# A two-layer hybrid backbone kernel: the list scheduler orders the instructions by its other model of times

## The chip, the cores and the metric

The kernel runs on one core of a Trainium2 chip. The metric is the device time of one execution in microseconds (us), as the median of several runs; lower is better. The engines are TensorE (PE; its weight loads are shown as PEld), VectorE (DVE), ScalarE (ACT) and GpSimd (POOL). Transfers are issued by SyncE (SP) and, for a few, by POOL. Each engine works through its own list of instructions in the order of the list, and so does the issue queue of SP.

## The reference

Two layers of a token backbone, one sample, 256 context tokens and 256 latent tokens, 1024 channels, all in fp32. Shortened:

```python
def trunk_layer(x_ctx, x_lat, c, c_ctx, ..., need_ctx, p):
    mod_lat = silu(c) @ w_mod + b_mod          # six rows: sh1, sc1, g1, sh2, sc2, g2
    mod_ctx = silu(c_ctx) @ w_mod + b_mod
    u = concat([x_ctx * (1 + sc1c) + sh1c, x_lat * (1 + sc1) + sh1])
    z_a, z_b, z_c, z_d = split_cols(u @ w_in)
    branches = (rwkv7_mixer(z_a), retention_mixer(z_b), hgrn2_mixer(z_c), gqa_mixer(z_d))
    merged = sum(sigmoid(u_rows @ w_gate[i]) * (branches[i] @ w_branch[i]) for i in range(4))
    mix = merged @ w_out
    x_lat = layer_norm(alpha * x_lat + g1 * mix[latent], ln1_g, ln1_b)
    ffn_lat = expert_choice_ffn(x_lat * (1 + sc2) + sh2, w_router, w_e1, w_e3, w_e2)
    x_lat = layer_norm(alpha * x_lat + g2 * ffn_lat, ln2_g, ln2_b)
    ...                                        # layer 0: the same for x_ctx
```

`expert_choice_ffn` lets each of 16 experts take its best tokens (a softmax of the router's logits, top-k), runs silu(x w_e1) * (x w_e3) through w_e2 and adds the results back. Layer 0 keeps all 512 tokens, layer 1 ("last") only the 256 latent ones. Each layer reads 192 MB of expert weights.

## The kernel before, in words

A Python program (class `Block`, called from `hybrid_block`) traces about 14,500 instructions, layer after layer. In a layer the stages follow one another: the modulation rows (`mod_product`, L261: a weight piece of 512 KB, `mw` or `y0`/`y1`, times the condition `sct`; in layer 0 half of the first row's products go to the tile `mod` and half to `m`); the projections and softmax attention, retention and HGRN (matmuls into `pj`, `g`, `y`; weights come by `wload`, L242, as `wr`, and are split by ACT and DVE or POOL into a high and a low half, `wh` and `wl`, for three-pass matmuls); RWKV, a long chain of small matmuls that need ACT and DVE between them, with a filler: the matmuls of the merge (`m<-mh,wh`, `m<-mh,wl`, `m<-ml,wh`) of the branches 3, 2, 1 and of the gate of branch 0, which a table of hooks (FILL) lets into the trace at chosen places of the chain.

The tail of a mixer is what the argument turns on. Its steps, with the names of layer 0 and, behind a slash, of layer 1: the last RWKV outputs (`y<-ar,st`), the group norm (`g<-y,cst` for mean, `g<-cst,sq` for variance), the transposes `g<-ident,rx`; from those the branch's output `y`, which ACT rounds to `yh` for the last merge (`m<-yh,wh`). With the transposes RWKV's buffers come free, and into them go the loads of w_out (`rows_in`, issued by POOL), of the residual `x`, of the router's weights `wrt` and of the first expert weights. Modulation rows are spread over the tokens by matmuls (`w<-rows,ident`), the router's constants are made from `wrt` (DVE: `wrb`, `wrr`) by `w_5948<-wrr` / `w_14246<-wrr`; then comes the last merge (`merge_last`), and the output projection (`h<-oh,mh`), logits, top-k and a gather.

The experts stream: one SP transfer per 1 MB unit (L1569), into a ring of rooms called ring, mid, low, late (and pair in layer 1). A room is refilled when the matmuls that read it are done, and SP issues its list in order, so a transfer whose room isn't free holds back all those behind it.

What sets the order: every instruction is traced in program order with its dependencies; `tile.TileContext` then plays the program against a model of how long each instruction takes and issues, for each engine, the earliest-traced instruction that the model calls ready. Tiles, buffers and addresses are fixed by the program; only the order of each engine's list comes from the model.

## Time and profile before

| | us |
|---|---|
| median of 3 runs | 2302.59 (2302.35 to 2312.79) |
| the profiled execution | 2311.96 |
| its span (1.76 lie outside it) | 2310.2 |
| PE busy in the span | 2048.9 |
| DVE, ACT, POOL busy | 1041.0, 627.2, 268.1 |
| granted TensorE clock, mean | 0.929 |

The profiled execution is 9.37 us above the median; it belongs with the slowest of the three runs. Times inside the execution are read from its trace, in us from the start of the span. A line such as "PE m L201" is an instruction recorded at line 201, which is a helper that all matmuls share, so stages are told apart by time and by tile name. An fp32 matmul shows as two records, an fp32r one as one.

### The profile page before, as it was taken

What the parts mean: (1) busy time and instruction counts of PE and PEld (TensorE: products, weight loads), DVE (VectorE), ACT (ScalarE), POOL (GpSimd) and SP (SyncE); (2) the same over time, 40 slices, a digit from 0 to 9 for tenths busy, and PEclk for the clock granted to TensorE, in tenths of its full rate; (3) what the DMA queues carried; (4) which work ended last, traced back from release to release, by engine and by line L of the source; (5) the groups of instructions that cost most, each with busy time, mean ns of one, the idle gap of its engine ahead of it and who ended that gap; (6) DMA issues with size and microseconds to landing.
All of it is one profiled execution on the core that took longest, in us unless ns stands there. A gap on an engine that the chain in (4) does not pass through costs nothing.

```text
span 2310.2 us, 37585 instructions
## 1 busy us (share of the span) xinstructions
PE 2048.9 (89%) x15964; PEld 1275.7 (55%) x15964; DVE 1041.0 (45%) x2179; ACT 627.2 (27%) x1039; POOL 268.1 (12%) x190
## 2 busy tenths in 40 slices
PE   6999999999999989999999899999889888766775
PEld 3657847677877744333332555868889654222222
DVE  3557755855532536222222557848664642010112
ACT  3353435422222212000000444555343320000000
POOL 2000111233332000000000200103353000000000
PEclk8999999999999989999999899998899988787777
DMA  8354242112124588999999646214222899999996
GB/s 317 97 194 155 64 142 73 41 58 70 56 66 184 201 351 326 422 425 425 426 426 425 220 138 211 69 47 165 92 93 86 338 372 424 424 425 423 424 425 288
DMA packets 96936, 554.85 MB, mean 240 GB/s; under 512 B 11296, under 2 KB 13280, under 8 KB 46848
## 3 DMA queue, kind: packets, MB, share of 16 engines
q1 hardware_dynamic: 95024, 541.83, 60.1%
q0 software_dynamic: 1200, 8.52, 0.9%
q8 instruction: 125, 2.05, 0.3%
q10 hardware_dynamic: 544, 2.10, 0.2%
q14 instruction: 43, 0.35, 0.0%
HBM read 549.13 MB, written 3.28 MB: 239 GB/s over the span
## 4 chain that ended last, share of the span: by engine, by line
PE 63%; DMA 22%; DVE 10%; ACT 2%; issue 2%; POOL 1%; SPq 0%; DVEq 0%; ACTq 0%; POOLq 0%
PE pj L201 14%; PE m L201 13%; PE h L201 12%; PE y L201 9%; DMA late<-in_w_e_dram 8%; PE g L201 6%; DMA mid<-in_w_e_dram 4%; DMA ring<-in_w_e_dram 4%; DMA pair<-in_w_e_dram 3%; PE mod L201 3%; PE w L201 3%; DMA mw<-in_wmod_dram 1%; DMA y<-in_wmod_dram 1%; DVE kb L186 1%; PE w L206 1%
## 5 line engine op out<-in xcount | busy, mean ns | idle before, releaser
L211 POOL TENSOR_TENSOR wl<-wr,wh 128x1280 fp32r<-128x1280 f32 (+1 forms) x62 | 177.7, 2867 | 292.6 <-ACT wh L183 266.2
L183 ACT ACTIVATE wh<-wr 128x1024 fp32r<-128x1024 f32 (+1 forms) x126 | 143.4, 1139 | 190.0 <-PE pj L201 86.4
L201 PE MATMUL m<-mh,wh 128*128 128x512 f32 (+1 forms) x512 | 183.4, 358 | 7.7 <-ACT th L183 7.7
L201 PE MATMUL m<-mh,wl 128*128 128x512 f32 (+1 forms) x512 | 179.4, 350 | 1.0 <-POOL wl L211 1.0
L201 PE MATMUL m<-ml,wh 128*128 128x512 f32 (+1 forms) x512 | 179.0, 350 | 0.0
L201 PE MATMUL h<-late,later 128*32 128x256 f32 (+1 forms) x880 | 143.1, 561 | 28.5 <-DMA late<-in_w_e_dram 28.5
L196 DVE SCALAR_TENSOR_TENSOR h<-h 128x512 f32<-128x512 f32 (+1 forms) x32 | 17.7, 555 | 313.9 <-ACT h L183 313.9
L211 DVE TENSOR_TENSOR wl<-wr,wh 128x1024 fp32r<-128x1024 f32 (+1 forms) x64 | 79.2, 1240 | 109.3 <-ACT wh L183 104.6
L183 ACT ACTIVATE h<-h 128x512 f32<-128x512 f32 (+1 forms) x32 | 15.7, 491 | 401.8 <-PE h L201 401.8
L201 PEld LDWEIGHTS m<-mh,wh 128*128 128x128 f32 x512 | 101.0, 197 | 25.7 <-ACT th L183 9.4
L186 DVE TENSOR_TENSOR h<-h 128x512 f32<-128x512 f32 (+1 forms) x32 | 17.7, 554 | 211.3 <-PE h L201 211.3
L201 PE MATMUL h<-ring,later 128*32 128x256 f32 (+1 forms) x640 | 93.6, 540 | 19.9 <-DMA ring<-in_w_e_dram 19.9
L201 PEld LDWEIGHTS m<-mh,wl 128*128 128x128 f32 x512 | 100.6, 196 | 13.8 <-issue 1.7
L201 PEld LDWEIGHTS h<-late,later 128*32 128x32 f32 (+1 forms) x880 | 45.5, 138 | 112.6 <-issue 63.4
L201 PEld LDWEIGHTS m<-ml,wh 128*128 128x128 f32 x512 | 100.8, 197 | 11.5 <-issue 1.6
L183 ACT ACTIVATE ht<-w 128x512 f32<-128x512 f32 (+1 forms) x32 | 15.7, 491 | 277.4 <-PE w L206 277.4
L201 PE MATMUL y<-late,ht 128*32 128x256 f32 (+1 forms) x536 | 73.5, 501 | 9.5 <-DMA late<-in_w_e_dram 6.9
L201 PE MATMUL h<-mid,later 128*64 128x512 f32 (+1 forms) x352 | 65.6, 569 | 9.0 <-DMA mid<-in_w_e_dram 9.0
L201 PEld LDWEIGHTS h<-ring,later 128*32 128x32 f32 (+1 forms) x640 | 30.1, 136 | 74.1 <-DMA ring<-in_w_e_dram 33.5
L201 PE MATMUL y<-ring,ht 128*32 128x256 f32 (+1 forms) x448 | 62.3, 526 | 9.7 <-DMA ring<-in_w_e_dram 6.3
L183 ACT ACTIVATE th<-m 128x512 f32<-128x512 f32 (+1 forms) x50 | 24.6, 492 | 164.6 <-PE m L201 164.6
L201 PE MATMUL pj<-mh,wl 128*128 128x512 f32 x152 | 61.9, 407 | 0.0
(629 smaller groups left out, 4480.5 us busy)
## 6 DMA issues: line engine op xcount, KB each, us to landing
late<-in_w_e_dram SPq DMA_DIRECT2D x144, 1024.0 KB, 19.5
ring<-in_w_e_dram SPq DMA_DIRECT2D x109, 1024.0 KB, 19.7
mid<-in_w_e_dram SPq DMA_DIRECT2D x63, 1024.0 KB, 19.7
pair<-in_w_e_dram SPq DMA_DIRECT2D x36, 1024.0 KB, 19.6
wr<-in_wmg_dram SPq DMA_DIRECT2D x48, 640.0 KB, 3.9
mw<-in_wmod_dram SPq DMA_DIRECT2D x48, 512.0 KB, 5.0
y<-in_wmod_dram SPq DMA_DIRECT2D x48, 512.0 KB, 4.0
low<-in_w_e_dram SPq DMA_DIRECT2D x20, 1024.0 KB, 19.8
```

Source lines behind the costliest of these rows:

```text
L183: self.nc.scalar.activation(out=out, in_=in_, func=func, **kw)
L186: self.nc.vector.tensor_tensor(out, a, b, op)
L196: self.nc.vector.scalar_tensor_tensor(out, a, s, b, op0, op1)
L201: self.nc.tensor.matmul(out, lhsT, rhs, start=start, stop=stop)
L206: self.nc.tensor.transpose(out, in_, self.ident[b:b + n, b:b + n])
L211: (eng or self.nc.vector).tensor_tensor(lo, src, hi.bitcast(F32), ALU.subtract)
```

## The change

One keyword at the place where the scheduler is made:

```diff
-    with tile.TileContext(nc) as tc:
+    with tile.TileContext(nc, schedule_with_timeline_sim=True) as tc:
```

With it the scheduler uses another model of the instruction times. The compiled program has the same instructions with the same names, operands and addresses (PE 10502, DVE 2141, POOL 195, SP 657 in both, ACT 1019 before and 1017 now, two activation-table loads fewer); what differs is the order of each engine's list, nearly everywhere a little. Three places matter below.

The first is SP's list in the experts of layer 0, where the weights of expert 3 are asked for. Before:

```order
L1569 DMA late6_7270<-in_w_e1_dram 128x2048
L1569 DMA late7_7272<-in_w_e1_dram 128x2048
L1569 DMA ring4_7274<-in_w_e1_dram 128x2048
L1569 DMA ring0_7276<-in_w_e3_dram 128x2048
L1569 DMA ring1_7278<-in_w_e3_dram 128x2048
L1569 DMA mid0_7280<-in_w_e3_dram 128x2048
L1569 DMA mid1_7282<-in_w_e3_dram 128x2048
```

Now:

```order
L1569 DMA late6_7270<-in_w_e1_dram 128x2048
L1569 DMA mid0_7280<-in_w_e3_dram 128x2048
L1569 DMA mid1_7282<-in_w_e3_dram 128x2048
L1569 DMA mid2_7284<-in_w_e2_dram 128x2048
L1569 DMA mid3_7286<-in_w_e2_dram 128x2048
L1569 DMA low0_7288<-in_w_e2_dram 128x2048
L1569 DMA late0_7290<-in_w_e2_dram 128x2048
L1569 DMA late7_7272<-in_w_e1_dram 128x2048
L1569 DMA ring4_7274<-in_w_e1_dram 128x2048
```

The six units into mid, low and late0, whose rooms the first matmuls of expert 2 leave, now stand ahead of late7, ring4, ring0 and ring1, whose rooms the second matmuls of experts 0 and 1 leave.

The second is PE's list at the tail of layer 0's mixer, a piece of the difference (`rx`: the normed RWKV output; `m_6119`, `m_6225`: merge matmuls of the gate and of the last merge; `w_5948`: the router's constants).

```order
 L201 MATMUL m_6119<-mh_109,wh_6115 128x512
 L201 MATMUL m_6119<-ml_110,wh_6115 128x512
+L206 MATMUL g_5861<-ident_91,rx_5839 128x128 x4
+L206 MATMUL g_5866<-ident_91,rx_5839 128x128 x4
 L201 MATMUL m_6119<-mh_109,wl_6116 128x512
...
 L201 MATMUL m_6225<-yh_6212,wh_6221 128x512
+L201 MATMUL w_5948<-wrr_5938,one_97 128x64
 L201 MATMUL m_6225<-yl_6211,wh_6221 128x512
```

Before, the transposes stood in the middle of the merge `m_5959` and the router's step in `m_6023`, five and four merges earlier; between the two stand now 53 merge matmuls and four `w<-rows` steps, before 42 and four.

The third is PE's list at the tail of layer 1's mixer. Before, around the transposes:

```order
L201 MATMUL m_14283<-ml_11007,wh_14279 128x256
L201 MATMUL m_14283<-mh_11006,wl_14280 128x256
L201 MATMUL m_14315<-mh_11006,wh_14311 128x256
L201 MATMUL m_14315<-ml_11007,wh_14311 128x256
L206 MATMUL g_14138<-ident_91,rx_14120 128x128 x2
L206 MATMUL g_14141<-ident_91,rx_14120 128x128 x2
L201 MATMUL m_14315<-mh_11006,wl_14312 128x256
L201 MATMUL m_14315<-mh_11006,wh_14311 128x256
```

Now:

```order
L201 MATMUL m_14379<-mh_11006,wl_14376 128x256
L201 MATMUL g_14121<-y0_8833,cst_9041 128x256
L201 MATMUL g_14129<-cst_9041,sq0_14118 128x2
L201 MATMUL g_14129<-cst_9041,sq1_14119 128x2
...
L206 MATMUL g_14138<-ident_91,rx_14120 128x128 x2
L206 MATMUL g_14141<-ident_91,rx_14120 128x128 x2
L201 MATMUL m_14419<-yh_14406,wh_14415 128x256
L201 MATMUL m_14430<-yh_14406,wh_14415 128x256
L201 MATMUL w_14212<-rows_9740,ident_91 32x256 x4
...
L201 MATMUL w_14225<-rows_9531,ident_91 128x512
...
L201 MATMUL w_14246<-wrr_14240,one_97 128x32
L201 MATMUL m_14419<-yl_14405,wh_14415 128x256
```

The gate's merges (`m_14315` to `m_14379`), which stood behind the transposes, now all stand ahead of the norm, and norm, transposes, the first use of `yh` and the router's step follow one another directly.

## Rows read from the trace of the kernel before

**Rows 1.** The page: the chain that ended last, by engine, share of the span.

```profile
PE 63%; DMA 22%; DVE 10%; ACT 2%; issue 2%; POOL 1%; SPq 0%; DVEq 0%; ACTq 0%; POOLq 0%
```

**Rows 2.** Busy time by stretch: stretch, length, engines (instructions), granted clock, DMA share, GB/s.

```profile
0.00:79.00 79.00, 58.81 (x325) 42.46 (x325) 29.91 (x64) 23.15 (x38) 13.46 (x19) 0.91 0.66 249
79.00:690.00 611.00, 589.76 (x4816) 420.45 (x4814) 363.21 (x729) 237.28 (x374) 111.31 (x70) 0.99 0.29 92
690.00:834.00 144.00, 125.01 (x585) 99.88 (x587) 65.92 (x133) 43.34 (x64) 14.99 (x8) 0.92 0.55 219
834.00:1276.00 442.00, 418.39 (x1924) 151.57 (x1922) 123.83 (x238) 38.50 (x70) 0.12 (x1) 1.00 0.99 407
1276.00:1780.00 504.00, 469.68 (x4508) 368.05 (x4505) 329.86 (x729) 222.25 (x371) 117.35 (x81) 0.95 0.37 122
1780.00:1863.00 83.00, 65.20 (x383) 52.20 (x381) 51.80 (x106) 32.48 (x53) 10.87 (x11) 0.88 0.79 316
1863.00:2310.20 447.20, 322.01 (x3432) 141.13 (x3432) 76.43 (x183) 30.21 (x71) 0.00 (x0) 0.77 0.96 401
```

**Rows 3.** The chain in order of time: start, us, what; ends of both expert stages.

```profile
1254.93 20.15 DMA late<-in_w_e_dram
...
1876.05 18.41 DMA mid<-in_w_e_dram
```

**Rows 4.** PE's longest waits: 79 to 330, 330 to 690, 1560 to 1780; total, times, longest.

```profile
PE mod L201 <- DMA y<-in_wmod_dram: 4.9, 4, 2.3
...
PE m L201 <- ACT th L183: 2.8, 1, 2.8
...
PE m L201 <- ACT th L183: 4.9, 3, 2.3
```

**Rows 5.** PE in order of time at layer 0's tail; idle before and releaser in brackets.

```profile
683.87 1.04 PE L206 MATMUL g<-ident,rx 128*128 128x128 f32 x8
...
691.37 1.98 PE L201 MATMUL w<-rows,ident 128*128 128x512 f32 x4 [1.69 <-ACT g L183]
...
704.35 0.66 PE L201 MATMUL w<-wrr,one 128*128 128x64 f32 x2 [3.98 <-DVE wrr L1443]
```

**Rows 6.** The same place by stretch, and two stretches of layer 0's experts.

```profile
706.00:711.00 5.00, 5.00 (x14) 3.88 (x14) 0.00 (x0) 0.00 (x0) 0.00 (x0) 0.56 0.49 197
711.00:735.00 24.00, 24.00 (x108) 19.85 (x107) 0.53 (x1) 7.73 (x10) 9.57 (x4) 1.00 0.44 175
880.00:916.00 36.00, 35.23 (x176) 15.51 (x178) 23.76 (x44) 4.30 (x8) 0.00 (x0) 1.00 0.78 289
916.00:1255.00 339.00, 321.34 (x1462) 110.40 (x1456) 85.95 (x166) 22.16 (x37) 0.12 (x1) 1.00 1.01 424
```

**Rows 7.** All engines in order of time at layer 1's tail.

```profile
1773.49 0.68 PE L201 MATMUL y<-ar,st 64*64 64x64 f32 x16
...
1781.33 0.70 PE L201 MATMUL g<-y,cst 128*128 128x256 f32 x2
...
1787.05 0.60 PE L206 MATMUL g<-ident,rx 128*128 128x128 f32 x4
...
1795.63 0.42 ACT L183 ACTIVATE yh<-y 128x256 fp32r<-128x256 f32 x1 [2.89 <-DVE y L186]
...
1797.74 0.36 DVE L1443 TENSOR_REDUCE wrr<-wrt 128x16 f32<-128x128 f32 x1
...
1820.02 0.80 PE L201 MATMUL h<-oh,mh 128*128 128x512 f32 x1 [3.10 <-ACT oh L183]
```

**Rows 8.** The start: SP's issues and the products that use the late ones.

```profile
19.47 8.81 SPq L261 DMA_DIRECT2D mw<-in_wmod_dram  x8
29.19 0.33 SPq L1753 DMA_DIRECT2D cst<-in_cst_dram  x1
...
36.86 2.97 SPq L261 DMA_DIRECT2D y<-in_wmod_dram  x2
...
44.94 3.63 PE L201 MATMUL m<-mw,sct 128*32 128x512 f32 x16
```

## The prediction

> **What bounds the kernel now.** I read the chain that ended last first: 63% of it is PE work and 22% transfers [rows 1]. Then busy time by stretch, since those shares mix stages [rows 2]. In both mixers PE is the bound: from 79 to 690 it works 589.76 of 611 us, from 1276 to 1780 469.68 of 504. A new order can't shorten that work, only the 21.2 and 34.3 us of idle time in it. From 834 to 1276, the experts of layer 0, both are near their end: PE works 418 of 442 us and the transfers fill 0.99 of the time; PE's own work then stops at 1254.93 and the last 20.15 us of the stage are a transfer [rows 3]. From 1863 on the transfers alone decide (0.96 of the time, PE 322 of 447 us), and the chain there is one row of transfers of some 20 us [rows 2, 3]. So a microsecond won or lost before 1863 moves the end by a microsecond, and inside layer 1's experts no order of the engines buys anything as long as the transfers follow each other without a gap. Between the stages lie two tails (690 to 834 and 1780 to 1863) where PE is idle for 19.0 and 17.8 us; they are chains through ACT, DVE and new loads.
>
> The question is therefore where PE's idle time goes, and whether a gap in the stream of weights closes. Instruction counts and sizes are the same, so there is no cost or gain of work except two activation-table loads on ACT, an engine that is busy for 27% and that I cost at nothing because PE or the transfers cover it.
>
> **The start.** SP's eight second transfers of the first modulation row (issued from 19.47) now stand behind cst, rot, gq, three rows of biases and constants, y0, y1 and one `wr`, which before were issued behind them, from 29.19 to 39.83 [rows 8]: up to 10.6 us later. PE in turn has all its other ready projections ahead of their products, which before ran in between and ended at 48.57 [rows 8]. The last issue was at 28.28; at 38.9 it would be in flight as long as the `y` pair, some 7 us, and its product would end about 2 us late. Two products of y0 and y1 behind it fill a later wait. I take +2 us, from 0 to +5.
>
> **The mixers.** In layer 0's attention PE waits 4.9 us in four places for `y` pieces of modulation weights [rows 4]. The new order spreads these products singly among projections where before they came in pairs, so the next load is asked for sooner; I take half, -2, with 0 and -4.9 as ends. In RWKV the long waits are for ACT (`th`, 2.8 us in layer 0 and 4.9 in three places in layer 1) [rows 4], with DVE's behind them. The new lists put more merge matmuls (0.22 us each, 108 in 24 us [rows 6]) ahead of a number of these chain steps. They also use them up: a merge that is moved ahead isn't there later, and I see steps set right behind their producers too. I take -3 in layer 0 and -4 in layer 1, where the idle time is the larger; the ends are zero and half of the idle time in each mixer, -10 and -17.
>
> **The tail of layer 0.** Transposes at 683.87; router's step at 704.35 after a wait of 3.98 us, and another wait of 1.69 us for a modulation row at 691.37 [rows 5]. The wait is followed by a granted clock of 0.56 from 706 to 711, in which 14 matmuls take the 5 us that 22 or so take afterwards [rows 6]; it costs some 2 us. In all 5.67 + 2, about 7.7 us. In the new order the 20.5 us from the transposes to the router's step (the load of `wrt` is issued when RWKV's buffers come free and lands behind larger loads) must be covered by 53 matmuls at 0.22 and four `w` steps, of which two took 1.98 [rows 5]: 11.8 + about 4 = 16 us. Some 4 us of waiting are left, instead of 7.7, and the modulation rows now have their inputs long before. I take -4. Ends: -7.7 (the load lands earlier, since nothing else is asked for there) and +3 (the wait is followed by the low clock again and the last merge is late).
>
> **Experts of layer 0.** From 880 to 916 the transfers move 289 GB/s, from 916 to 1255 424 [rows 6]: 36 x (1 - 289/424) = 11.5 us of transfer time are lost, because late7 and what stands behind it wait for rooms that experts 0 and 1 leave with their second matmuls. Now the six units into mid, low and late0 go first. PE, too, runs first matmuls of experts 2 and 3 before the second ones of 0 and 1. The transfers' 20.15 us at the end [rows 3] show that they are last, so a gap closed here comes back at the end of the stage. But PE works 35.23 of those 36 us [rows 6]: rooms can't come free sooner than PE's work lets them, and units set ahead of a free room block it. I take half, -6, with 0 and -11.5 as ends. Later swaps in SP's list meet a stream without gaps and cost nothing.
>
> **The tail of layer 1.** Here the order does harm. In the list before, the gate's merges stand behind the norm and the transposes and cover both. Now they all stand ahead. From the last RWKV outputs (done at 1774.2) to the transposes (1787.05) PE never waited; of this the norm's second mean (1781.33) to the transposes is 5.7 us [rows 7]. With merges ahead of it, the last outputs come some 8 us of PE work later. Behind them, PE's work up to the transposes is 15 us, and waits of the norm, bare now, of about 4 us are added: 19 instead of 13. From the transposes on, `yh` is complete 8.6 us later (1795.63 + 0.42 - 1787.4) and `wrr` 10.7 us later (1797.74 + 0.36) [rows 7]. PE has some 4 us of work (two matmuls, eight small and two large `w` steps) ahead of the router's step, so it waits 6 to 7 us. Some 11 us of last merges and norm rows follow, and the 3.1 us for `oh` [rows 7] stay: 10.7 + 11 + 3.1 = 25 us, where before it were 1820.02 - 1787.4 = 32.6. Sum: +8 + (19 - 13) + (25 - 32.6) = +6.4. The matmuls behind a wait of 6 to 7 us will start at the low clock, as after 704.35, for some 2 us more. I take +8. Ends: +2 (`wrt` lands earlier) and +14 (the loads of w_out aren't there in time, or the clock stays low for the whole tail: 11 us of work doubled). It is paid in full, since the room of the first stalled expert transfer waits for layer 1's first expert matmuls, and from there the stream has no gap.
>
> On the clock this row can be held against a page: in this trace the granted clock was 0.56 behind a wait of 4 us, so near the lower level of 1.2 GHz, and 1.00 from 711 on [rows 6]. The Trainium skill (TensorE: Matmul & The Clock Gate, What's actually happening) says that there are just these two levels, 1.2 and 2.4 GHz, and that the engine is taken down when it has been idle; by it a list with a long bare chain is worse than its waits alone say. The trace agrees at this place. If all work of the tail ran at the low level, the term were +14 instead of +8, as its upper end says.
>
> **Sum.** +2 - 2 - 3 - 4 - 6 - 4 + 8 = -9 us; layer 1's start and attention, where waits of `mod` products change places, I leave at zero. Against the profiled execution that is 2312 - 9 = 2303; the median stands 9.4 us lower and I carry the difference over to it: 2302.6 - 9 = 2293.6, forecast 2294.
>
> **The rivals.** *Slower by bare chains* (chance 0.25). One mechanism: the model takes ACT, DVE and loads for faster than they are, so steps stand directly behind their producers where the list before had work between them. Layer 1's tail is the place where it is plainly seen (0.8 us of PE work between mean and transposes where 5.7 us passed before). If it rules in RWKV as well, the idle 21.2 and 34.3 us of the mixers [rows 2] grow by a third instead of shrinking: +18 instead of -9 for mixers; with the tails at +14 and 0, experts at -6 and the start at +2 the sum is +28, 2331; at half of it 2316. It decides when RWKV waits more than before; for it speaks layer 1's tail, against it that merges stand ahead of the chain in both RWKV stages, a sign of a model that takes the chain for slow.
>
> *More gained* (0.2). The model is the better one all along: the `y` waits go (-4.9), RWKV loses half its idle time (-8, -12), layer 0's tail -7.7, the gap of transfers closes (-11.5), layer 1's tail +8, start 0. The sum is -36: 2267. For it speaks that each of these waits has work of PE in the list that could cover it; against it that PE's work is the same, and cover spent early is missing later.
>
> *Nothing changes* (0.1). PE is 96% busy in the first mixer and the transfers 0.96 in the last stage [rows 2]; new waits replace old ones one for one: 2303.
>
> The forecast's own mechanism, a small net gain, has 0.45, with 2282 to 2306 as its own range.
>
> **Range and chances.** A measurement of this kernel can't tell less than 0.5% (11.5 us) from no change. The two outer cases have 0.45 together; leaving out the lower third of one and the upper half of the other gives 2269 to 2321. Of the forecast's 0.45, 0.14 lies below 2291, 0.29 within, 0.02 above 2314. Of the slower rival 0.20 is over 2314 and 0.05 within. Of the larger gain 0.19 is faster and 0.01 within; no change has 0.10 within. So faster 0.33, same 0.45, slower 0.22.
>
> **What would show it.** In the trace of the changed kernel: the last `m<-mw,sct` of the start ends near 50 (start); fewer than 4 us of PE's waits on `y<-in_wmod` (attention); the sum of PE's idle time in each RWKV stretch (if it grows, the rival of bare chains); at layer 0's tail one wait of about 4 us for `wrr` in place of two (if none, the loads came early); the stretch between expert 2 and 3 above 350 GB/s, and the last transfer of layer 0's stage 6 us earlier relative to the stage's start; at layer 1's tail a wait of 4 us between mean and transposes and one of 6 to 7 us behind them, with a clock below 0.9. The forecast falls if RWKV's idle time changes by more than 10 us in either layer, or if a transfer set ahead of its room holds back the stream in layer 1, which I cost at nothing.

## The result and the profile after

| | us |
|---|---|
| before, median of 4 runs | 2303.68 (2302.35 to 2312.79) |
| after, median of 4 runs | 2337.41 (2332.29 to 2341.49) |
| ratio after to before | 1.0135, 95% interval 1.011 to 1.016 |
| the profiled execution of after, its span | 2332.29, 2330.5 |

The change costs 33.7 us by the medians, 1.35% by the ratio. The profiled execution of after is the fastest of its runs, and that of before, as said ahead of the prediction, one of its slowest, so the two shown traces stand only 20.3 us apart. I therefore took a second profile of the kernel before (run `e0_before` below, span 2304.8), which is a typical one, and set after against that.

The same pieces of work in both: layer 0's mixer (from the first use of a modulation row to the first output projection `h<-oh,mh`), layer 0's experts (to the residual of the next layer), layer 1's mixer (from its first `mod<-mw,sct` to `h<-oh,mh`), and the rest from layer 1's gather on. Columns as in [rows 2], the engines in the order PE, PEld, DVE, ACT, POOL. First `e0_before`:

```profile
48.60:746.70 698.10, 667.76 (x5211) 484.67 (x5211) 397.24 (x803) 270.42 (x424) 131.54 (x81) 0.99 0.31 100
813.70:1268.80 455.10, 431.06 (x2003) 161.12 (x2003) 129.34 (x253) 42.16 (x78) 0.12 (x1) 1.00 0.98 404
1283.40:1816.10 532.70, 493.27 (x4702) 390.97 (x4702) 340.39 (x753) 233.48 (x398) 128.11 (x88) 0.95 0.39 130
1857.00:2304.80 447.80, 313.89 (x3434) 136.63 (x3434) 76.82 (x185) 30.22 (x71) 0.00 (x0) 0.80 0.96 402
```

The kernel after, the same four pieces:

```profile
49.40:761.80 712.40, 685.43 (x5210) 497.21 (x5210) 391.12 (x801) 265.56 (x422) 133.68 (x81) 0.96 0.30 98
826.40:1275.10 448.70, 424.72 (x2002) 161.22 (x2002) 129.41 (x253) 42.24 (x78) 0.12 (x1) 0.99 0.99 409
1290.90:1838.80 547.90, 498.88 (x4703) 400.29 (x4703) 343.45 (x753) 234.21 (x399) 129.15 (x88) 0.92 0.37 125
1881.30:2330.50 449.20, 312.98 (x3434) 135.64 (x3434) 76.21 (x185) 30.18 (x71) 0.00 (x0) 0.79 0.95 397
```

Layer 0's mixer is 14.3 us longer (712.4 for 698.1), layer 0's experts 6.4 shorter (448.7 for 455.1), layer 1's mixer 15.2 longer (547.9 for 532.7), the last stage 1.4 longer; the four pieces between make up +1.2, and the sum is the 25.7 us between the spans. Where in the mixers? Idle time of PE (length less busy time) goes from 30.3 to 27.0 us in layer 0 and from 39.4 to 49.0 in layer 1. The rest, 17.7 us in layer 0 and 5.6 in layer 1, is *busy* time, with the same matmuls: PE worked more slowly. The granted clock says so too (0.96 for 0.99, 0.92 for 0.95). Against the first profile of the kernel before, with other shares by layer (busy 672.5 of 704.5 us in layer 0, 490.8 of 528.5 in layer 1), it is 21.0 us of busy time in a loss of 27.3.

Stretch by stretch this is HGRN, whose small matmuls (`g<-e`, `m<-e`, 64 rows by 128) run among wide ones (128x512 or 128x256: projections `pj`, merges). After, a stretch with the full clock, the long one behind it, the passage from HGRN to RWKV (421 to 437), and two of layer 1's HGRN:

```profile
293.00:315.00 22.00, 22.00 (x113) 14.06 (x111) 16.20 (x36) 4.91 (x6) 2.86 (x3) 1.00 0.26 87
315.00:351.00 36.00, 30.51 (x128) 19.07 (x128) 16.56 (x46) 12.81 (x25) 3.45 (x7) 0.72 0.07 23
421.00:437.00 16.00, 14.60 (x53) 11.02 (x54) 8.29 (x26) 10.42 (x17) 1.65 (x3) 0.57 0.01 2
1474.00:1492.00 18.00, 14.07 (x60) 10.84 (x59) 9.64 (x30) 8.75 (x15) 1.57 (x3) 0.62 0.10 30
1504.00:1523.00 19.00, 14.64 (x60) 9.70 (x57) 5.97 (x15) 4.61 (x11) 2.21 (x4) 0.64 0.09 28
```

The same part of HGRN in `e0_before`, up to the first RWKV norm of layer 0, and in layer 1:

```profile
293.00:318.00 25.00, 24.84 (x156) 15.93 (x155) 12.81 (x32) 8.17 (x17) 3.74 (x5) 1.00 0.41 127
318.00:370.00 52.00, 52.00 (x228) 27.57 (x227) 26.15 (x55) 26.72 (x41) 2.20 (x6) 1.00 0.28 87
1465.00:1500.00 35.00, 33.75 (x239) 26.60 (x238) 21.94 (x58) 17.86 (x32) 4.20 (x9) 1.00 0.21 61
```

Before, PE is busy all through with the clock at 1.00: 156 records in 25 us. After, the 36 us from 315 hold 128 records and no wide projection until 350.7: from 314.95 on there are 76 records of 64-row matmuls in a row, where the list before has at most 32 in this part. Layer 1 has 44 in a row from 1503.6 on, before at most 16. The wide projections that stood between them in the list before stand ahead of 315 and behind 350 now. PE also waits in these stretches, 6.2 us from 290 to 350 and 8.4 from 1440 to 1530, for tiles of HGRN that come from DVE and ACT (the longest; total, times, longest one):

```profile
PE g L201 <- DVE e L186: 3.8, 3, 2.6
...
PE m L201 <- DVE al L1183: 1.9, 1, 1.9
...
PE g L201 <- ACT rsr L183: 1.6, 1, 1.6
```

In `e0_before` the same stretches have waits of 0.2 and 2.2 us in all. The other places of the prediction, in after. First single rows of PE in order of time (idle before and releaser in brackets): the end of the start's last products; layer 0's tail (the transposes, the router's step, the output projection); layer 1's tail (variance, transposes, router's step, output projection).

```profile
47.52 1.05 PE L201 MATMUL m<-mw,sct 128*32 128x512 f32 x4 [0.22 <-DMA mw<-in_wmod_dram]
...
728.53 1.03 PE L206 MATMUL g<-ident,rx 128*128 128x128 f32 x8
...
748.60 0.33 PE L201 MATMUL w<-wrr,one 128*128 128x64 f32 x2
...
761.83 0.50 PE L201 MATMUL h<-oh,mh 128*128 128x512 f32 x1 [1.56 <-ACT oh L183]
...
1811.19 1.05 PE L201 MATMUL g<-cst,sq 128*128 128x2 f32 x8 [1.53 <-ACT sq L183]
...
1813.67 1.11 PE L206 MATMUL g<-ident,rx 128*128 128x128 f32 x4 [1.42 <-ACT rx L183]
...
1823.20 0.30 PE L201 MATMUL w<-wrr,one 128*128 128x32 f32 x2
...
1838.77 0.80 PE L201 MATMUL h<-oh,mh 128*128 128x512 f32 x1 [4.59 <-ACT oh L183]
```

Then by stretch, the larger part of layer 0's RWKV and the place in the experts that had the gap:

```profile
490.00:728.00 238.00, 237.22 (x2722) 190.86 (x2721) 102.74 (x178) 67.56 (x90) 76.84 (x32) 1.00 0.20 65
...
880.00:916.00 36.00, 36.00 (x176) 19.52 (x174) 15.37 (x30) 9.78 (x21) 0.00 (x0) 1.00 0.99 417
```

And PE's waits for `th` in layer 1's RWKV, 1560 to 1800:

```profile
PE m L201 <- ACT th L183: 9.1, 4, 4.7
```

### The profile page after: what moved, and what is told of

It is laid out like the page before. It is cut to its first block, busy times and chain, and to the rows that moved or that the text cites. A ratio compares the mean times of both kernels' runs of the same rounds, so it can differ in the third digit from the quotient of the medians.

```text
span 2330.5 us, 37558 instructions
## 1 busy us (share of the span) xinstructions
PE 2052.8 (88%) x15964; PEld 1290.7 (55%) x15964; DVE 1037.8 (45%) x2179; ACT 621.1 (27%) x1037; POOL 271.6 (12%) x190
## 4 chain that ended last, share of the span: by engine, by line
PE 60%; DMA 26%; DVE 9%; ACT 2%; issue 2%; SPq 0%; POOL 0%; DVEq 0%; POOLq 0%; ACTq 0%
PE pj L201 15%; PE m L201 14%; PE h L201 10%; PE y L201 8%; DMA late<-in_w_e_dram 8%; PE g L201 6%; DMA mid<-in_w_e_dram 6%; DMA ring<-in_w_e_dram 4%; DMA pair<-in_w_e_dram 3%; PE mod L201 3%; PE w L201 3%; DMA mw<-in_wmod_dram 2%; DVE kb L186 1%; DMA sct<-sd 1%; DVE tmp L186 1%
## 5 line engine op out<-in xcount | busy, mean ns | idle before, releaser
L201 PE MATMUL h<-late,later 128*32 128x256 f32 (+1 forms) x880 | 130.5, 542 | 33.0 <-DMA late<-in_w_e_dram 33.0
L196 DVE SCALAR_TENSOR_TENSOR h<-h 128x512 f32<-128x512 f32 (+1 forms) x32 | 17.7, 553 | 270.3 <-ACT h L183 270.3
L186 DVE TENSOR_TENSOR h<-h 128x512 f32<-128x512 f32 (+1 forms) x32 | 17.7, 554 | 212.6 <-PE h L201 212.6
L201 PE MATMUL h<-ring,later 128*32 128x256 f32 (+1 forms) x640 | 88.4, 548 | 24.9 <-DMA ring<-in_w_e_dram 24.9
L201 PE MATMUL h<-mid,later 128*64 128x512 f32 (+1 forms) x352 | 60.7, 579 | 17.2 <-DMA mid<-in_w_e_dram 17.2
L201 PE MATMUL pj<-mh,wh 128*128 128x512 f32 x152 | 62.9, 414 | 0.0
## 6 DMA issues: line engine op xcount, KB each, us to landing
late<-in_w_e_dram SPq DMA_DIRECT2D x144, 1024.0 KB, 19.5
```

The lines of the kernel that those rows point to most:

```text
L186: self.nc.vector.tensor_tensor(out, a, b, op)
L196: self.nc.vector.scalar_tensor_tensor(out, a, s, b, op0, op1)
L201: self.nc.tensor.matmul(out, lhsT, rhs, start=start, stop=stop)
```

## The experiments

Each run was measured beside runs of the kernel before on the same chip; the ratio is to those, with its 95% interval. In most of them the order of some engines is fixed by a helper that is called once the program is traced. It ties each instruction of a list to the one ahead of it in that list, so nothing but the order changes. The lists that it doesn't fix are made anew by the scheduler around those that it does. Where it fixes nearly all lists as in the kernel before (e16 below), the time is that of before, so the helper itself costs nothing that shows. The edits are shown shortened:

```diff
         hybrid_block(tc, args, out)
+        force_order(tc)
```

### How far the kernel before varies: e0_before

No edit.

> The kernel before once more, unchanged, for a second profile of it. The profiled execution shown ahead of the prediction took 2311.96 us, 9.4 above the median, so a trace of a usual execution is missing. Theory: the 9 us lie in one place that the new order doesn't touch (start, or transfers of an expert stage), so the difference of the two kernels by stage stays +8 us in layer 0's mixer, -7 in its experts and +19 in layer 1's mixer. Rival: they are spread over the mixers, which then are 9 us shorter in a usual execution, and the loss by stage is larger than the two traces at hand say.

Measured: 2305.32 us, ratio 0.9993 (0.9967 to 1.0019); the span of its profile is 2304.8. Single executions of the kernel before lie between 2294 and 2317, and between its two profiles layer 0's mixer differs by 6.4 us (shorter here) and layer 1's by 4.2 (longer here). So neither the theory nor the rival holds as it stood: the two profiles differ in the mixers, one way in layer 0 and the other way in layer 1. A difference of a few us between stages of two single profiles is not taken for an effect below.

### Which layer, which engine: e2_l0_old, e3_l1_old, e1_pe_old, e12_helpers_old

```diff
 e2: changed scheduler
+    lists of all engines: layer 0 of before, layer 1 of after
 e3: changed scheduler
+    lists of all engines: layer 0 of after, layer 1 of before
```

> Layer 0 with the lists of before on every engine, layer 1 with those of the changed kernel. The two traces give +19.4 us from layer 1's start to its output projection, and 0 for layer 0 as a whole. Theory: about 2304 + 20 = 2324 or more. Rival (the loss is in layer 0 and the traces hide it, since the one of before is a long execution): near 2305.

> The complement: layer 0 with the lists of the changed kernel on every engine, layer 1 with those of before. Theory: 2304 within 4 us, since in layer 0 the mixer's loss (+8 at the output projection) is given back by the experts (-7). Rival: 2315 to 2335.

Measured: e2 2326.41 us, ratio 1.0084 (1.0057 to 1.0111); e3 2310.62, ratio 1.0027 (1.0005 to 1.005). For e2 the theory holds; e3 lies between theory and rival, 3 us above the one and 4 below the other. So layer 1 costs some 20 us and layer 0 some 6, in which 14 us of loss in the mixer and 6 to 7 of gain in the experts lie one upon the other.

```diff
 e1: changed scheduler
+    list of PE: before
 e12: changed scheduler
+    lists of DVE, ACT and POOL: before
```

> The changed kernel, with PE's list alone put back into the order of before by issue-order edges; ACT, DVE, POOL and SP are ordered by the changed model around it. Theory (the loss is PE's order: steps of the chains set bare, where PE then waits and its clock falls): the time is that of before, 2304, within 6 us. Rival (the loss comes from the lists of the other engines, SP's or DVE's): it stays at 2330 to 2340.

> The mirror of the run with PE's old list: the changed scheduler, with the lists of DVE, ACT and POOL forced to the order of the kernel before in both layers, while PE's and SP's lists come from the new model under that. In the changed kernel HGRN's tiles e come some 20 us later than before, when PE has used up its wide work. Theory (what brings HGRN late is the order of the helping engines): HGRN's results come as early as before, the runs of bare small matmuls with a granted clock near 0.50 are gone, 2305 to 2318. Rival 1 (PE's own list puts its wide work too early, whatever the helpers do): the low clock in HGRN stays, 2325 to 2340. Rival 2 (no engine's list can be taken from the other order): above 2340, as with PE's old list (2358).

Measured: e1 2358.04, ratio 1.0229 (1.0185 to 1.0274); e12 2462.61, ratio 1.0693 (1.0669 to 1.0717). Both are slower than before and after alike; for e12 the second rival holds, and for e1 what was expected of it fell altogether. Here the lists of some engines are good only together with the lists that were made with them, so these two runs name no engine's list as "the bad one", and they say nothing on HGRN.

### HGRN's own order or what stands between: e4_att_old, e5_att_new

```diff
 e4: changed scheduler
+    attention, retention, HGRN: in themselves as before; RWKV, tails, experts: as after
 e5: scheduler of before
+    attention, retention, HGRN: in themselves as after; RWKV, tails, experts: as before
```

> The changed kernel, with the instructions of the attention, retention and HGRN part of both layers (those traced before RWKV) in the order of the kernel before, on every engine; RWKV, tails and experts in the order of the changed kernel. Theory: the loss sits in HGRN's small matmuls, which the new lists leave without wide projections between them. Then the time falls from 2337 by about 30 us, to 2296 to 2310, the matmuls m<-e of layer 1 take 6 to 7 us again instead of 15.0, and the granted clock of HGRN's stretch is 1.00 or near it. Rival 1: the loss sits behind HGRN (RWKV, tail, their bare waits) and HGRN only shows a clock that was lost for other reasons: the time stays above 2325. Rival 2: lists of two orders do not fit at their seams, as where PE's list alone was set back (2358): above 2340.

> The complement: the kernel before, with attention, retention and HGRN of both layers in the order of the changed kernel on every engine, and RWKV, tails and experts as before. Theory (HGRN left bare): slower than before by 25 to 35 us, 2328 to 2340, with m<-e of layer 1 at 13 us or more. Rival 1 (the loss sits behind HGRN): 2300 to 2312. Rival 2 (seams): slower than 2340, and with waits at the passage to RWKV.

Measured: e4 2320.41, ratio 1.0067 (1.0043 to 1.0091), between the theory and the first rival; e5 2343.82, ratio 1.0169 (1.0143 to 1.0195), some 4 us above the theory's range and by its number a case of the second rival too; `m<-e` of layer 1 takes 13.3 us (from start to start, waits left out, 80 records; 6.1 in `e0_before`, 15.0 in after), as the theory asked, and 7.4 in e4. That time is no measure of the loss, though: in e4 it is nearly back and layer 1's mixer is not, and in e5, where it is long, layer 1's mixer is only 6.7 us longer than in `e0_before` (539.4), while layer 0's is 25.8 longer (723.9). In e4 each part keeps its own order, but how HGRN and RWKV's projections are laid into each other is still the new model's. The small matmuls run bare there as well, at other places:

```profile
305.00:327.00 22.00, 20.62 (x78) 13.28 (x79) 6.02 (x15) 5.08 (x13) 2.62 (x5) 0.53 0.32 95
1500.00:1524.00 24.00, 21.09 (x63) 11.96 (x64) 7.40 (x21) 8.30 (x17) 0.35 (x4) 0.58 0.11 33
```

Layer 1's mixer is no shorter than in after (548.2 us); layer 0's, 705.9, is near the longer of the two profiles of before (704.5). So, by e4 and e5 alike, in layer 1 it is not the order within HGRN that costs but what lies between its steps.

### The bare runs themselves: e7_spread, e14_even

```diff
 L201 MATMUL g<-q,th 128x128 x4
+L201 MATMUL pj<-mh,wh 128x512
+L201 MATMUL pj<-ml,wh 128x512
+L201 MATMUL pj<-mh,wl 128x512
 L201 MATMUL g<-e 128x128 x4
+L201 MATMUL pj<-mh,wh 128x512
+L201 MATMUL pj<-ml,wh 128x512
+L201 MATMUL pj<-mh,wl 128x512
 L201 MATMUL m<-e 128x128 x4
```

> The changed kernel with PE's list changed at three places in HGRN's stretch and nowhere else: 48 wide projection matmuls of layer 0 and 45 of layer 1, which stood just ahead of the runs of small matmuls without any wide one between them, are spread over those runs, three behind every four small ones. No work is added or left out; the other engines' lists come from the same model and differ only where the moved products are used. Theory (small matmuls left bare run at the lower clock and wait for DVE and ACT unhidden): of the 74 us of these runs (granted clocks 0.72, 0.64, 0.73) some 14 us of idle time and up to 21 us of low clock are at stake; 2310 to 2325, with a granted clock near 1.00 there. Rival (wide work is only moved from one place to another, what it hides here is missing there): 2331 to 2340.

Measured: 2319.7 us, ratio 1.0073 (1.0055 to 1.0091): 17.7 us less than after, about half of the loss, by an order of PE at three places and without any work taken away. In layer 0 the low stretch is gone but for some 3 us, although PE still waits there (3.0 us for `e`, 2.2 in one piece); in layer 1 it is not. Yet the two mixers of its profile are shorter than in after by about as much, 4.8 us in layer 0 (707.6) and 4.5 in layer 1 (543.4), so the profiles don't say in which layer the gain lies:

```profile
305.00:346.00 41.00, 39.23 (x192) 23.72 (x190) 21.66 (x54) 13.70 (x26) 3.60 (x7) 1.00 0.07 20
1490.00:1514.00 24.00, 20.52 (x71) 12.96 (x71) 7.84 (x19) 5.05 (x11) 1.99 (x5) 0.57 0.07 23
```

If wide work between the small matmuls were all, more of it should help layer 1:

```diff
 all wide projections of HGRN's stretch (197 in layer 0, 193 in layer 1)
-    in the groups of the changed kernel's list
+    spread evenly behind every four small matmuls
```

> The changed kernel with PE's list changed in HGRN's stretch of both layers: all wide projection matmuls between 230 and 351 us (197, with 223 small ones) and between 1443 and 1529 us (193, with 122 small ones) of the changed kernel's trace are spread evenly behind every four small ones, none earlier than it stood; no work is added, and the other engines' lists come from the same model. Where three wide ones stood behind every four small ones, layer 0's stretch came back to a clock of 1.00, layer 1's did not. Theory (what the changed lists lack in HGRN is wide work between the small matmuls, and layer 1 wants more of it): the low stretches of layer 1 in HGRN are gone, its mixer takes 530 to 537 us instead of 548, and the sum is 2303 to 2314. Rival (in layer 1 it is the waits for e, which more wide work ahead of them does not cover): the mixer stays at 543 or more, 2316 to 2326.

Measured: 2361.83, ratio 1.0247 (1.0218 to 1.0276), 24 us slower than after. Theory and rival both fell; it is slower than either said, in layer 0's mixer (724.6 us for 712.4) and in layer 1's (568.3 for 547.9). The low clock of layer 1 stays (first row), with six wide matmuls behind every four small ones. In layer 0 a new low stretch begins behind one wait of 5.39 us (for `lga`, ending at 241.3) and lasts 26 us without another wait, with three or four wide ones behind every four small ones (second row). And even at a clock of 1.00 (third row) the work takes longer:

```profile
1462.00:1490.00 28.00, 26.78 (x103) 19.38 (x104) 14.82 (x43) 9.74 (x21) 3.51 (x5) 0.51 0.00 1
239.00:267.00 28.00, 25.70 (x96) 19.40 (x96) 19.67 (x52) 9.33 (x18) 3.87 (x3) 0.52 0.16 53
270.00:350.00 80.00, 79.12 (x411) 49.07 (x411) 42.74 (x97) 29.58 (x49) 7.18 (x9) 1.00 0.30 94
```

At the prices that the same matmuls have in `e0_before` (the time from each start to the next, waits left out), the work of 290 to 350 in e14 is worth some 49 us; it took 59. Single rows show why. At full clock wide matmuls follow each other every 0.23 us and the records of small ones every 0.11 (eight records are four matmuls). At each change between them both sides take longer:

```profile
300.03 0.40 PE L201 MATMUL pj<-ml,wh 128*128 128x512 f32 x1
300.36 1.16 PE L201 MATMUL g<-e 64*128 64x128 f32 x8
301.44 0.50 PE L201 MATMUL pj<-mh,wh 128*128 128x512 f32 x1
301.77 0.39 PE L201 MATMUL pj<-ml,wh 128*128 128x512 f32 x1
302.01 0.40 PE L201 MATMUL pj<-mh,wl 128*128 128x512 f32 x1
```

From 300.03 to the first small one 0.33 us instead of 0.23, then 1.08 us for eight small records, the first and the last of which take 0.21 and 0.20 (medians of the stretch) instead of 0.11, and 0.33 from the first wide one to the next. One excursion costs 0.4 us, and from 290 to 350 there are 23. Groups of `g<-e` and `m<-e` are also parted that overlap where one stands right behind the other: in `e0_before` 16 such records take 1.64 us (300.92 to 302.56), where two groups of eight apart take twice 1.08. So groups that are cut finely pay for the change of form. That e7's gain is what is left after such a price is likely, but not shown.

### The clock alone: e8_warm, e9_warm_before

```diff
                 ps = self.cyc("g", "m")
+                for _ in range(2 if p == 1 else 0):
+                    self.nc.tensor.matmul(ps[:, 0:512], self.uh[:, 0, 0:128], self.uh[:, 0, 0:512], start=True, stop=True)
```

> The changed kernel in its own order on every engine, plus 40 extra wide matmuls per layer: ahead of each group of small matmuls of HGRN's second half stand two products of 128x512 of the layer's input by itself, written to the place that the small ones then overwrite. At 0.22 to 0.23 us each that is 9 us more of PE work in each layer, 18 in all. Theory (the clock is the larger part of the loss): the granted clock of HGRN's runs comes back towards 1.00, the small matmuls take their short time again (m<-e of layer 1 below 9 us instead of 15.0), and of the 18 us little is to be seen: 2325 to 2342. Rival (the waits are the larger part, the clock only goes with them): the extra work is paid, less what it puts into waits: 2345 to 2356.

> The control: the kernel before, in its own order on every engine, with the same 40 extra wide matmuls per layer at the same groups. Here HGRN's clock is 1.00 without them, so they can give nothing back. Both theories: 2304 plus 12 to 18, so 2316 to 2322. By the theory of the clock the distance of the changed kernel to the kernel before then falls from 34 us to below 22 between these two; by the rival it stays about 34.

Measured: e8 2349.19, ratio 1.019 (1.0165 to 1.0214); e9 2341.59, ratio 1.017 (1.0147 to 1.0192). The distance between the two is 7.6 us where it was 33.7, as the theory of the clock had it. By stage it shrinks in layer 1's mixer alone, from 15.2 us to 2.1 (550.6 and 548.5 us); in layer 0's it is 11.7 (728.4 and 716.7) where it was 14.3. And e8's own sum, 2349, is the rival's. The theory's sign of `m<-e` isn't there: in layer 1 of e8 it takes 14.8 us (from start to start, 80 records), about as in after. The clock, which that time doesn't measure, is low there for 10 us (last two rows), for 27 in two stretches in after; and layer 0 has a low stretch in which PE works without a pause. The control, too, was mis-sized, 2342 for 2316 to 2322: an extra product costs 0.31 us amid small ones (12.5 us for 40), not 0.23, and lengthens those behind it. So this pair doesn't decide. Layer 0 and layer 1 in e8:

```profile
318.00:327.00 9.00, 8.38 (x52) 6.10 (x51) 7.58 (x22) 2.50 (x3) 0.85 (x1) 1.00 0.17 58
327.00:347.00 20.00, 20.00 (x56) 12.90 (x56) 6.18 (x15) 3.99 (x12) 1.18 (x2) 0.50 0.00 0
1495.00:1508.00 13.00, 11.05 (x37) 7.53 (x38) 7.15 (x24) 4.85 (x10) 1.02 (x2) 0.61 0.15 42
1508.00:1545.00 37.00, 34.94 (x164) 23.97 (x163) 14.76 (x38) 10.07 (x22) 3.09 (x7) 1.00 0.08 29
```

And in e9, layer 0's groups:

```profile
297.00:334.00 37.00, 37.00 (x188) 22.90 (x186) 14.32 (x33) 9.60 (x18) 2.17 (x5) 1.00 0.31 89
```

### What a wait costs: e10_wait_small, e11_wait_wide, e13_wait_string

```diff
 e10, e13 (HGRN, last levels of its second half)
+    nc.gpsimd.tensor_copy(e[:, 0, :n], e[:, 0, :n])
 e11 (one projection weight of RWKV in each layer)
+    nc.gpsimd.tensor_tensor(l[:, :n], w, h[:, :n], ALU.subtract)
```

> The price of one wait among small matmuls. The kernel before in its own order on every engine; in HGRN's second half, at the last level, POOL copies the tile e onto itself three times in layer 0 and five times (half as wide) in layer 1, so that PE, which in the trace of the kernel before has at most 0.3 us to spare there, waits some 3 us once in each layer. Theory (a wait among small matmuls costs several times its length, because the granted clock falls behind it and stays low while small matmuls follow): behind each wait 10 to 20 us at a clock near 0.50, which cost 5 to 9 us on top of the 3; for two waits 2304 plus 16 to 24: 2320 to 2328. Rival (a wait costs its length and some 2 us for the clock, as the forecast had it for layer 0's tail; the low clock of the changed kernel is due to something else in its list): 2304 plus 8 to 12: 2312 to 2316.

> The same wait among wide matmuls. The kernel before in its own order on every engine; POOL computes the low half wl of one projection weight of RWKV again (three times in layer 0, twice in layer 1), which delays it by some 6.5 and 4.5 us at places where PE has 3.6 and 0.8 us to spare, so that PE waits some 3 us once in each layer amid projections of 128x512. Both theories: the waits themselves, 6 to 7 us in all. Theory: the clock comes back within 5 us, since wide matmuls follow: 2304 plus 8 to 12: 2312 to 2316. Rival (a wait costs the same wherever it lies): the same sum as where the wait lies among small matmuls, within 4 us.

Measured: e10 2313.46, ratio 1.0045 (1.0025 to 1.0064); e11 2323.36, ratio 1.0066 (1.0043 to 1.009). The waits were 3.1 and 1.9 us in e10, 5.2 and 4.6 in e11. Behind each the clock is low for 3 to 7 us, among small matmuls as among wide ones. e10 from the end of the wait on, in layer 0 and in layer 1:

```profile
304.00:310.00 6.00, 5.98 (x32) 3.42 (x34) 2.41 (x7) 1.26 (x2) 1.18 (x2) 0.72 0.41 126
310.00:330.00 20.00, 20.00 (x106) 11.41 (x105) 6.35 (x17) 7.05 (x17) 0.14 (x2) 1.00 0.30 93
1497.00:1504.00 7.00, 7.00 (x24) 4.47 (x21) 4.62 (x10) 1.74 (x5) 1.26 (x2) 0.52 0.09 8
```

e11 in layer 0:

```profile
391.00:396.00 5.00, 5.00 (x13) 4.01 (x14) 1.22 (x2) 0.00 (x0) 0.10 (x1) 0.57 0.70 262
396.00:420.00 24.00, 22.57 (x126) 16.28 (x127) 16.86 (x36) 12.54 (x20) 7.95 (x5) 1.00 0.18 56
```

For e10 the rival holds. e11 lies above both ranges, because its waits are longer; by the price of a wait it is a case of the rival too. e10 costs 9.6 us for 5.0 us of waits, 2.3 us more for each; e11, by its ratio, 15.2 for 9.8, 2.7 more for each, and by its median 19.5 (its waits are 4.6 and 5.2 us where I had set some 3). A wait alone costs its length and some 2 to 5 us, wherever it lies, about what the forecast had taken for layer 0's tail. The low stretches of HGRN in after last 14 to 20 us each (0.72 over 36 us is 20 us at 0.50) and need something more.

> A string of waits in place of one. The kernel before in its own order on every engine; POOL copies e onto itself five, five and two times at the last three levels of HGRN's second half, about 1.0 us each in layer 0 and 0.4 in layer 1, so that PE waits at each of three levels that follow one another within some 20 us, 6 us in all in layer 0 and 4 in layer 1. One wait alone cost its length and left the clock low for 4 to 8 us. Theory (waits that follow one another hold the clock down, and that is what the changed kernel has in HGRN, three or four of them in each low stretch): one low stretch of 12 us or more in each layer, 2304 plus 10 plus 12 or more: above 2326. Rival (wide work between the small matmuls brings the clock back after each wait; the changed kernel lacks that work): at most 5 us of low clock behind each wait, 2304 plus 10 plus 3 to 8: 2317 to 2322.

Measured: 2321.03, ratio 1.006 (1.0043 to 1.0078). The string came about in layer 1 only (1.15 and 3.42 us, 7.5 us apart; in layer 0 one wait of 0.53 was left). Behind it the clock was at 0.52 for 6 us and at 1.00 from 1506 on, as behind a single wait. So waits at three levels one behind another, which the theory wanted, were not tested. The number is the rival's, but not by its sum: these waits and their clock make up some 8 us of a loss of 14 by the ratio and 17 by the medians, and the others, which lie elsewhere, I can't assign.

### The other terms by themselves: e6_exp_new, e15_tail0_new, e16_tail1_new

```diff
 scheduler of before
+    e6:  layer 0's experts as after
+    e15: layer 0's tail (from RWKV's norm on) and experts as after
+    e16: layer 1's tail (from RWKV's norm to the route's end) as after
```

> The kernel before, with only layer 0's experts in the order of the changed kernel, on every engine. Theory: the six units that are asked for ahead close the gap in the stream of weights, and the stage from the route's end to the layer's end falls from 455 us to 448: 2296, 7 us faster, resolved by five rounds if it is so. Rival: the stage was shorter in the changed kernel because its transfers began earlier relative to the route's end; then the order alone gives 0 to 2 us, 2301 to 2304.

> The kernel before, with the tail of layer 0's mixer (from RWKV's norm on) and layer 0's experts in the order of the changed kernel on every engine, all else as before. The experts alone gave 2298. Theory (the forecast's terms for the two places hold and can be had without HGRN's loss): the waits of 1.69 and 3.98 us in the tail and the low clock behind them are gone, 4 to 7 us, so 2291 to 2295. Rival (the new tail needs the new list ahead of it; the merges that cover it there have been used up here): waits of the tail in other places, 2297 to 2303.

> The kernel before, with only the tail of layer 1's mixer (from RWKV's norm to the route's end) in the order of the changed kernel on every engine: the gate's merges ahead of the norm, and norm, transposes, the first use of yh and the router's step bare. The forecast put this at +8 (+2 to +14): 2306 to 2318, with waits of some 4 us between mean and transposes and 6 to 7 us behind them. Rival (the changed kernel's trace shows waits of only 3 and 3 us there and the output projection 25 us behind the transposes, where it was 33 before, so that the two cancel): 2301 to 2306.

Measured: e6 2298.32, ratio 0.9964 (0.9949 to 0.998); e15 2287.52, ratio 0.9922 (0.9901 to 0.9943); e16 2307.67 beside 2307.32, ratio 1.0009 (0.9988 to 1.003). In e15 the tail from the transposes to the output projection, layer 0's experts, and the stretch with the gap; in e16 the rows of layer 1's tail:

```profile
707.30:742.00 34.70, 30.61 (x123) 22.72 (x121) 23.21 (x36) 15.01 (x24) 6.42 (x5) 0.95 0.69 277
806.50:1256.10 449.60, 424.63 (x2003) 161.43 (x2003) 129.42 (x253) 42.23 (x78) 0.12 (x1) 0.99 0.99 408
868.00:900.00 32.00, 32.00 (x164) 17.20 (x160) 15.40 (x29) 6.84 (x15) 0.00 (x0) 1.00 0.96 396
```

```profile
1781.71 1.05 PE L201 MATMUL g<-cst,sq 128*128 128x2 f32 x8 [1.53 <-ACT sq L183]
...
1784.19 0.66 PE L206 MATMUL g<-ident,rx 128*128 128x128 f32 x4 [1.42 <-ACT rx L183]
...
1787.99 0.79 PE L201 MATMUL m<-yh,wh 128*128 128x256 f32 x2 [3.15 <-ACT yh L183]
...
1808.55 0.74 PE L201 MATMUL h<-oh,mh 128*128 128x512 f32 x1 [4.59 <-ACT oh L183]
```

e6 lies 2 us above its theory and 3 below its rival; against the kernel before beside it, it is 7.8 us faster, about the theory's 7. For e16 the number itself is in the theory's range, but the change against the kernel before is nothing, as the rival had it. e15 is faster than both kernels, by 18 us (0.8%) against the kernel before, and 3.5 us below the theory's range: layer 0 up to the output projection takes 694.0 us (698.1 in `e0_before`), the route 64.5 (67.0), the experts 449.6 (455.1). These three are 12 us. The rest of the 20.5 us between the spans lies in layer 1's mixer (524.9 us; 532.7 and 528.5 in the two profiles of the kernel before), whose order is not changed, and I don't put it down to the edit.

## Why the prediction was wrong, step by step

**The failed step** is a premise ahead of the sum: "A new order can't shorten that work, only the 21.2 and 34.3 us of idle time in it." I read PE's busy time in [rows 2] as a fixed amount. It can grow: of the 29.5 us that the two mixers lost, 23.3 are busy time (17.7 + 5.6). The mixers' terms (-2, -3, -4, together -9) were made of waits alone, and HGRN, which has no long wait in [rows 4], got no term at all. Its stretch has a clock of 0.99 [rows 2] while wide work lies between its small matmuls, and I didn't ask what would become of it when the order moves that work. The mixers as measured above hold the tails too: -5 was forecast for them (-9, and -4 and +8 for the tails) and +29.5 measured, 34.5 of the 43 us by which the median missed. Most of the rest is that these two profiles lie 8 us nearer to each other than the medians.

**The rival of bare chains** came nearest: steps that stand bare, with no other work between them and their producers. But I looked for them in RWKV and the tails, and priced them as idle time (+18). The place was HGRN, and the larger part of the price PE's slower work. That the model takes the helping engines for too fast, as I gave for a reason, no run shows. 2337 lies above its 2331 and 16 us above the range.

**Start**, +2: the last products end at 47.52 + 1.05 = 48.57 in both [rows 8]; 0, within the ends.

**Layer 0's attention**, -2: the waits for `y` are 5.9 us (3 times, longest 3.4) instead of 4.9 [rows 4]. No gain shows (4.0 us in `e0_before`); that products which are spread singly ask for the next piece sooner is not borne out.

**RWKV**, -3 and -4: in layer 0 the waits are gone from 490 to 728 (237.22 of 238 us busy), more than forecast, but one of 4.5 us for `kb` stands ahead of that, at 455.7, where the list before had two of 2.7 in all. In layer 1 the `th` waits grew from 4.9 [rows 4] to 9.1. The forecast's own sign for its fall, more than 10 us of change in RWKV's idle time, did not show (against the first profile some 4 us less in layer 0, 5 more in layer 1); the fall came from elsewhere.

**Layer 0's tail**, -4: the gain is nearer to the lower end, -7.7. Neither the wait for a modulation row nor that for `wrr` [rows 5] is left; the router's step starts at 748.60 with no wait ahead of it, and the clock is 1.00 from 728 to 762. By itself (e15) the tail with its route is worth 6.6 us by the stages of its profile (4.1 + 2.5), and e15 is 0.4% faster than e6, which has the experts alone.

**Layer 0's experts**, -6: right. One reading behind it was not: PE's work does not stop at 1254.93, it goes on to the stage's end with waits of under 1 us for transfers; [rows 3] only say that the chain runs through the transfer there. The gap [rows 6] is closed, 417 GB/s from 880 to 916 for 289; the stage is 6.4 us shorter in after, 5.5 in e15, and alone it made the kernel faster by 0.2 to 0.5%.

**Layer 1's tail**, +8: the mechanism is there, the size is not. Mean to transposes, I put waits of 4 us, they are 1.53 and 1.42; behind the transposes 6 to 7, it is 2.93 in after and 3.15 in e16, both for `yh`, and neither has a wait for `wrr`. From transposes to output projection I had 25 us; 25.1 (1838.8 - 1813.7) were measured, and 24.4 in e16. The merges set ahead (+8) and missing behind the transposes (-7.6) cancel, as the sum had it; mis-sized is what it added on top, 6 us of bare chain and 2 for the clock. e16 puts the whole at 0 (-3 to +7).

**The bound**: that a microsecond ahead of layer 1's experts moves the end by a microsecond holds. Layer 1's route ends 24.3 us later than in `e0_before`, and the end is 25.7 later.

**The clock.** The prediction drew on the Trainium skill (TensorE: Matmul & The Clock Gate, What's actually happening), by which activity of the engine releases the clock and idleness takes it down. The two levels are what the rows show. That the engine's being busy is enough is not: in e8 PE is busy for 20.00 of 20 us at 0.50 (a busy time whose ends are modelled), and in after for 30.51 of 36 at 0.72, while a list with the same small matmuls and wide ones in groups has 1.00. The measurement decides.

**What stays open**: what exactly holds the clock down for 14 us and more at a time in HGRN, and with it how the 21 to 23 us of busy time come about; e7 shows by an experiment that about half of the loss hangs on how small and wide matmuls alternate there, the other half is placed in HGRN by the traces alone. Waits by themselves don't hold the clock down (e10, e11, e13: 3 to 7 us). More wide work alone doesn't bring it back: spreading it did in layer 0 (e7) but not in layer 1 (e7, e14). In after both come together, small matmuls bare and several waits of 0.5 to 2.6 us among them. But a string of waits isn't needed: one of 0.6 us was enough in e8's layer 0 (20 us of low clock behind it) and one of 5.4 us in e14's (26 us). What sets these two apart from e10, e11 and e13 is what follows the wait, groups of four small matmuls with two to four wide ones between them, where the list before follows in the others. In the list before wide matmuls stand between HGRN's levels in groups; no run here varied the size of the groups at a given amount of wide work and without waits.

## What to carry to other kernels

Before you treat an engine's busy time as fixed under a new order, look where its small instructions run and what stands between them: on TensorE the same matmuls took 13 to 18 us longer in one mixer. Judge a new order stage by stage and keep the stages that gain: here the order of one tail and one expert stage gave 0.8%, while the whole new order lost 1.35%. And take the lists of all engines of a stage together: against the kernel before, PE's old list without the others' cost 2.3%, those of DVE, ACT and POOL without PE's 6.9%.

## What the runs showed of the hardware

- TensorE at a granted clock of 0.50 for 20 us without a pause in its work, after a wait of only 0.6 us (e8, 327 to 347), as small matmuls of 64 rows ran with two wide ones ahead of each group of four.
- Behind a single wait of 5.4 us the clock stayed at 0.50 for 26 us without another wait, as groups of four small matmuls and of three or four wide ones alternated (e14, 241 to 267).
- In the list before, a single wait of 1.9 to 5.2 us left the clock low for 3 to 7 us, whether small or wide matmuls followed (e10, e11).
- A change between wide matmuls and small ones of 64 rows and back costs 0.4 us at full clock (e14), and one wide product of 128x512 amid small ones 0.31 us, where it takes 0.23 among its like (e9).
